# More staging, value and bias-table tiles around the attention; modulation sums without a cleared accumulator, closed three steps later

## The chip, the cores and the metric

The kernel runs on one core of one Trainium2 chip. The metric is the device time of one execution in microseconds (us), taken as the median of several runs. Before the change it is 2842.87 us, the median of 3 runs between 2839.62 and 2844.02 us.

Names of the engines: PE is TensorE (matmuls; PEld are its weight loads), DVE is VectorE, ACT is ScalarE, POOL is GpSimd, SP is SyncE, which here only issues DMAs. SPq and ACTq are the DMA queues that SP and ACT feed.

## The reference, cut to what matters

The model has two layers over 256 latent tokens and 256 context tokens with 2048 features, all in float32. Every layer first turns a conditioning vector into six modulation vectors of 2048 values:

```
sh1, sc1, g1, sh2, sc2, g2 = split(silu(c) @ ada_w[l] + ada_b[l], 6)
h = rmsnorm(x) * (1 + sc1) + sh1
layer 0: y = concat(gated_delta_net(h, ctx), neighbourhood_attention(h, ctx)) @ w_out
layer 1: y = (gate_b * conv3(gate_c * val)) @ w_out
x = x + g1 * y
x = x + g2 * swiglu(rmsnorm(x) * (1 + sc2) + sh2)
out = rmsnorm(x)
```

The gated-DeltaNet half has 8 heads. For each it inverts 64x64 triangles and then runs a recurrence over chunks, forward and backward, first over the context and then over the latent tokens. The attention half has 8 heads: 256 queries against 256 latent keys within a window, with a learned bias table (`ev_rpb`), and against 256 context keys, in one softmax.

## The kernel before, in words

**Matmuls.** Every weight matrix comes from HBM in tiles of 128x1024 float32 (`raw`, L226, four buffers in layer 0's first half). ACT makes a rounded copy `whi` (L169), DVE the remainder `wlo` (L238), and PE multiplies three of the four products of the high and low parts (L284 to L295 and L309 to L313). These streams are called QB, KB, VB, ZA, W_out and so on by the columns of the weight matrix.

**Modulation vectors.** The six vectors of layer 0 that are not needed at once, and those of layer 1, are summed in the background by `ada_job`. For a block of columns (512 wide in layer 0's first half, 1024 wide later) POOL clears `acc` (128 x width, L327), a DMA puts the bias of the block in its first row (L328), and 16 steps follow: a DMA loads `araw` (L331, three buffers for the narrow form), and DVE adds `araw` times a column of silu(c) to `acc` (L332). Then the block is closed at once: PE sums `acc` over the partitions. For 512 columns these are 4 products with a column of ones (L338); for 1024, `acc` is split into high and low part and goes through 16 products (L346), and ACT takes the row out of PSUM (`grow`). There are 12 narrow and 14 wide blocks.

**Staging.** The streams QB, KB and VB end in `stage`: ACT or DVE copies a 128x512 result out of PSUM into a tile `nst` (L1050, L164, L166), and an ACT queue DMA stores it in HBM (L1051). ZA does the same with `zst` (L1118 to L1121), under the same tag. There are `NST` = 2 such tiles.

**Attention.** Per head, `na_scores` loads the windows of the bias table with two DMAs on the ACT queue into `br` (one buffer, L1081), DVE adds the band mask and writes `bq` (two buffers, L1084), and PE forms the scores (L1088) and adds the bias (L1089). `na_values` loads `vb` (two buffers, L1103) and forms the output (L1112).

**Recurrence.** A latent step is, on PE, state times keys (L918), state times queries (L927), `xdT` times `R` (L938), in some steps the state update (L946), and `AT` times `vn` (L960). Between them DVE makes `R` (L921) and ACT makes `vd` and `vn` (L942, L956).

**What sets the order.** Nothing in the program fixes the order of an engine's instructions: a scheduler with its own timeline puts them in order when the kernel is built, by what each needs and when its buffer comes free. Each engine then executes its list strictly in that order, so an instruction that waits holds all behind it, and so does a DMA issue in its queue.

Of the kernel before, what the change touches and what calls it, by code (L numbers as in the profile page):

```python
# [23 lines left out]
F32 = mybir.dt.float32  # L24
F32R = mybir.dt.float32r
AF = mybir.ActivationFunctionType
OP = mybir.AluOpType
AX = mybir.AxisListType

D = 2048  # L30
KT = D // 128
# [8 lines left out]
GH = 6  # L40
YO = (2, 0, 1, 3)
NPT = 1
AB = 3
R_QB = 1.2
R_KB = 1.8
R_ZA = 1.8
R_WO = 2.0
NST = 2
TAIL = 2
HEAD = 2  # L50
PO = 96
# [54 lines left out]
def body(tc, x, c, ctx, c_ctx, ada_w, ada_b, norm_mix, norm_ffn, ffn_w_gate, ffn_w_up, ffn_w_down,  # L106
# [3 lines left out]
    PE, ACT, DVE, POOL, SP = nc.tensor, nc.scalar, nc.vector, nc.gpsimd, nc.sync  # L110
# [43 lines left out]
    def smt():  # L154
        small.append(small.pop(0))
        return small[0].tile([128, 512], F32, name="sm", tag="sm")
# [11 lines left out]
    def acopy(dst, src):  # L168
        ACT.activation(dst, src, AF.Copy)  # L169
# [12 lines left out]
    ident = C("ident")  # L182
    pick = cpool.tile([128, 15], F32R, name="pick")
    ones = C("ones")

    def transpose(dst, src):
        n = src.shape[0]
        return PE.transpose(dst, src, ident[:n, :n])  # L188

    cT = cpool.tile([128, 32], F32, name="cT")  # L190
# [6 lines left out]
    gcol = {}  # L197
    row_d = {}
# [118 lines left out]
            yield  # L317


    def ada_job(pool_, l, seg, kind, gamma=None, width=1024, bufs=2):  # L320

        wr = ada_w[l].rearrange("(k p) n -> p k n", p=128)
        nf = width // 128
        for blk in range(D // width):
            c0 = seg * D + blk * width
            acc = pool_.tile([128, width], F32, name="acc", tag="acc", bufs=1)
            POOL.memset(acc, 0.0)  # L327
            SP.dma_start(acc[0:1, :], ada_b[l:l + 1, c0:c0 + width])  # L328
            for k in range(KT):
                raw = pool_.tile([128, width], F32, name="araw", tag="araw", bufs=bufs)  # L330
                SP.dma_start(raw, wr[:, k, c0:c0 + width])  # L331
                DVE.scalar_tensor_tensor(acc, raw, cT[:, k:k + 1], acc, op0=OP.mult, op1=OP.add)  # L332
                yield
            fs_ = slice(blk * nf, (blk + 1) * nf)
            p = smt()
            if width < 1024:
                for f in range(nf):
                    PE.matmul(p[:, f:f + 1], acc[:, f * 128:(f + 1) * 128], ones[:, 0:1], start=True, stop=True)  # L338
                pc = p
            else:  # L340
                ah = pool_.tile([128, width], F32R, name="ah", tag="ah", bufs=1)
                al = pool_.tile([128, width], F32R, name="al", tag="al", bufs=1)
                split(ah, al, acc, DVE)
                for f in range(nf):
                    for a in (ah, al):
                        PE.matmul(p[0:nf, 0:128], pick[:, nf - 1 - f:2 * nf - 1 - f], a[:, f * 128:(f + 1) * 128],  # L346
                                  start=f == 0 and a is ah, stop=f == nf - 1 and a is al)
                g = pool_.tile([16, 128], F32, name="grow", tag="grow", bufs=1)[0:nf]
                acopy(g, p[0:nf, 0:128])
                if kind == "row":  # L350
                    ACT.dma_start(row_d[l, seg][fs_], g)
                    continue
                pc = smt()
                transpose(pc[:, 0:nf], g)
            if kind == "sc":
                DVE.scalar_tensor_tensor(scc[l, seg - 1][:, fs_], pc[:, 0:nf], 1.0, gamma[:, fs_], op0=OP.add, op1=OP.mult)
            else:
                DVE.tensor_copy((shc if kind == "sh" else gcol)[l, seg][:, fs_], pc[:, 0:nf])
        if kind == "row" and width < 1024:
            p = smt()  # L360
            transpose(p[0:16, 0:128], gcol[l, seg])
            g = pool_.tile([16, 128], F32, name="grow", tag="grow", bufs=1)
            DVE.tensor_copy(g, p[0:16, 0:128])
            SP.dma_start(row_d[l, seg], g)

    def load_row(l, seg):
        r = rpool.tile([128, D], F32, name="row", tag="row", bufs=1)
# [3 lines left out]

    class Pump:
        def __init__(self, jobs, steps, total):
            self.it = (s for j in jobs for s in j)
            self.rate = total / max(steps, 1)
            self.due = 0.0
            self.done = False
# [62 lines left out]
    p = smt()  # L440
# [621 lines left out]
    nap = pool("na", stack=nastk)  # L1062
# [3 lines left out]
    bandf = C("band")  # L1066
# [6 lines left out]
    def na_scores(h):  # L1073
        kb = nap.tile([128, 512], F32, name="kb", tag="kb", bufs=2)
        qb = nap.tile([128, 256], F32, name="qb", tag="qb", bufs=2)
        bq = nap.tile([128, 6, 64], F32, name="bq", tag="bq", bufs=2)
        br = nap.tile([128, 6, 64], F32, name="br", tag="br", bufs=1)
        for half in range(2):
            src = bass.AP(tensor=ev_rpb.tensor, offset=ev_rpb.offset + h * 465 + (5 - half) * 31 + 15 - 63,
                          ap=[[1, 64], [31, 6], [1, 64]])  # L1080
            ACT.dma_start(br[half * 64:half * 64 + 64], src)  # L1081
        SP.dma_start(kb, kb_d[:, h, :])
        SP.dma_start(qb, qb_d[:, h, :])
        DVE.tensor_tensor(bq, br, bandf[:, None, :].to_broadcast([128, 6, 64]), op=OP.add)  # L1084
        out_ = []
        for t in range(2):
            p = nat(h)
            PE.matmul(p, qb[:, t * 128:(t + 1) * 128], kb, start=True, stop=False)  # L1088
            PE.matmul(p[:, 0:256], C("flip"), bq[:, 2 - 2 * t:6 - 2 * t, :].rearrange("p s c -> p (s c)"),  # L1089
                      start=False, stop=True)  # L1090
            s = nap.tile([128, 512], F32, name="s", tag="s", bufs=4)
            m = nap.tile([128, 1], F32, name="m", tag="m", bufs=4)
            DVE.tensor_reduce(m, p, axis=AX.X, op=OP.max, negate=True)
            l = nap.tile([128, 1], F32, name="l", tag="l", bufs=4)
            ACT.activation(s, p, AF.Exp, bias=m, accum_out=l)
            DVE.reciprocal(l, l)
            DVE.tensor_scalar(s, s, l, None, op0=OP.mult)
            out_.append(s)
        return out_

    def na_values(h, ss):
        vb = nap.tile([128, 4, 128], F32, name="vb", tag="vb", bufs=2)
        SP.dma_start(vb, vb_d[:, :, h * 128:(h + 1) * 128])  # L1103
        PT = nap.tile([128, 4, 256], F32, name="PT", tag="PT", bufs=NPT)
        for t in range(2):
            pt = nat(h)
            for j in range(4):
                transpose(pt[:, j * 128:(j + 1) * 128], ss[t][:, j * 128:(j + 1) * 128])
            copy(PT[:, :, t * 128:(t + 1) * 128], pt.rearrange("p (j q) -> p j q", j=4))
        po = nat(h)  # L1110
        for j in range(4):
            PE.matmul(po[:, 0:256], vb[:, j, :], PT[:, j, :], start=j == 0, stop=j == 3)  # L1112
        split(yhi[2 + h // 4][:, h % 4, :], ylo[2 + h // 4][:, h % 4, :], po[:, 0:256])
# [98 lines left out]
    row = []  # L1212
# [191 lines left out]
```

## Time and profile before

| | |
|---|---|
| median of 3 runs | 2842.87 us (2839.62 to 2844.02) |
| the profiled execution | 2848.17 us, span 2846.4 us |
| PE busy in the span | 2732.5 us, 96% |
| DVE, ACT, POOL busy | 68%, 46%, 2% |
| mean granted TensorE clock | 0.986 of full speed |

The span is what the profiler saw from the first instruction to the last. The profiled execution takes 1.8 us more than its span and lies 5.3 us above the median. A "busy" matmul is counted with its pipeline, and its end is modelled, so PE may lose a little more than its idle time says. In square brackets behind a row stands how long the engine was idle before it and what released it.

### The profile page before, as it was taken

To read this page: it belongs to the slowest core of one execution; us is meant where nothing else is said; L and a number is where in the kernel's file an instruction comes from. 1 tells how busy PE (TensorE), PEld (TensorE's weight loads), DVE (VectorE), ACT (ScalarE), POOL (GpSimd) and SP (SyncE) were. 2 spreads that over 40 slices of the span, in tenths; PEclk is the share of its full clock that TensorE was granted. 3 is DMA by queue.
4 is the path that set the end of the run, shared out by engine and by line. 5 is a ranking of instruction groups with operands and counts; after the bars stand their busy time and mean duration, and the time that the engine had idled before them with its cause. 6 is when DMAs were issued, how large, how long until landed. Compare 5 with 4: busy or idle time off the path is not lost.

```text
span 2846.4 us, 40363 instructions
## 1 busy us (share of the span) xinstructions
PE 2732.5 (96%) x15113; PEld 2281.6 (80%) x15113; DVE 1924.8 (68%) x2647; ACT 1308.3 (46%) x1945; POOL 51.1 (2%) x77
## 2 busy tenths in 40 slices
PE   5999999989989999999999999999999999999998
PEld 3699989888767778888888878878878888888886
DVE  3387767857667878776677768897678644445665
ACT  3267543222354544444445545444454444444554
POOL 0000001000000000000000000000000000000000
PEclk9999999999999999999999999999999999999999
DMA  9955568777758599987788657998559766656653
GB/s 345 311 177 164 143 208 253 243 225 236 210 170 278 200 318 346 347 285 249 272 305 282 198 175 243 328 319 306 179 179 332 262 188 180 195 186 215 192 192 126
DMA packets 284927, 680.78 MB, mean 239 GB/s; under 512 B 57273, under 2 KB 97313, under 8 KB 283323
## 3 DMA queue, kind: packets, MB, share of 16 engines
q1 hardware_dynamic: 262148, 652.48, 69.4%
q10 hardware_dynamic: 22583, 25.73, 3.0%
q8 instruction: 118, 1.93, 0.3%
q14 instruction: 78, 0.64, 0.1%
HBM read 657.63 MB, written 20.48 MB: 238 GB/s over the span
## 4 chain that ended last, share of the span: by engine, by line
PE 70%; DMA 15%; DVE 9%; issue 3%; ACT 2%; SPq 1%; POOL 0%; ACTq 0%; DVEq 0%; POOLq 0%
PE mm L287 17%; PE mm L285 17%; PE mm L284 17%; DMA araw<-in_ada_w_dram 11%; PE mm L313 7%; DVE acc L332 3%; DVE wlo L238 3%; PE sm L188 2%; PE mm L293 2%; PE mm L295 2%; PE mm L294 2%; DMA raw<-in_od_w_in_dram 1%; DMA acc<-in_ada_b_dram 1%; PE gd L477 1%; ACT whi L169 0%
## 5 line engine op out<-in xcount | busy, mean ns | idle before, releaser
L238 DVE TENSOR_TENSOR wlo<-raw,whi 128x1024 fp32r<-128x1024 f32 x800 | 971.5, 1222 | 452.3 <-ACT whi L169 446.3
L169 ACT ACTIVATE whi<-raw 128x1024 fp32r<-128x1024 f32 x800 | 841.9, 1058 | 875.5 <-PE mm L287 632.4
L332 DVE SCALAR_TENSOR_TENSOR acc<-araw,cT,acc 128x1024 f32<-128x1024 f32 (+1 forms) x416 | 431.2, 1037 | 228.4 <-DMA araw<-in_ada_w_dram 198.8
L285 PE MATMUL mm<-wlo,fhi 128*128 128x512 f32 x1232 | 473.6, 394 | 0.2 <-DVE wlo L238 0.2
L284 PE MATMUL mm<-whi,fhi 128*128 128x512 f32 x1232 | 470.9, 396 | 0.6 <-ACT fhi L1187 0.6
L287 PE MATMUL mm<-whi,flo 128*128 128x512 f32 x1232 | 392.2, 392 | 0.1
L284 PEld LDWEIGHTS mm<-whi,fhi 128*128 128x128 f32 x1232 | 232.4, 189 | 50.4 <-ACT fhi L1187 1.0
L287 PEld LDWEIGHTS mm<-whi,flo 128*128 128x128 f32 x1232 | 231.0, 188 | 50.7 <-DVE flo L1189 0.3
L285 PEld LDWEIGHTS mm<-wlo,fhi 128*128 128x128 f32 x1232 | 232.5, 189 | 48.7 <-DVE wlo L238 0.7
L284 PE MATMUL mm<-whi,ahi 128*128 128x512 f32 x672 | 259.8, 392 | 0.0
L285 PE MATMUL mm<-wlo,ahi 128*128 128x512 f32 x672 | 259.4, 391 | 0.0
L287 PE MATMUL mm<-whi,alo 128*128 128x512 f32 x672 | 209.7, 392 | 0.0
L313 PE MATMUL mm<-hllo,whi 128*128 128x256 f32 x640 | 181.1, 287 | 0.0
L313 PE MATMUL mm<-hlhi,wlo 128*128 128x256 f32 x600 | 169.4, 288 | 2.0 <-issue 1.5
L313 PE MATMUL mm<-hlhi,whi 128*128 128x256 f32 x600 | 167.5, 290 | 1.0 <-DVE hlhi L502 1.0
L172 ACT ACTIVATE ahi<-prodT 128x256 fp32r<-128x256 f32 x176 | 73.0, 417 | 194.7 <-PE mm L285 187.6
L285 PEld LDWEIGHTS mm<-wlo,ahi 128*128 128x128 f32 x672 | 126.2, 188 | 27.5
L284 PEld LDWEIGHTS mm<-whi,ahi 128*128 128x128 f32 x672 | 126.2, 188 | 27.2
L287 PEld LDWEIGHTS mm<-whi,alo 128*128 128x128 f32 x672 | 126.1, 188 | 27.3
L285 PE MATMUL mm<-wlo,dhi 128*128 128x512 f32 x336 | 127.3, 398 | 2.6 <-DVE wlo L238 2.4
L313 PEld LDWEIGHTS mm<-hllo,whi 128*128 128x128 f32 x640 | 124.0, 194 | 0.4
L284 PE MATMUL mm<-whi,dhi 128*128 128x512 f32 x336 | 123.5, 396 | 0.3 <-DVE u_t L1329 0.3
(399 smaller groups left out, 4055.9 us busy)
## 6 DMA issues: line engine op xcount, KB each, us to landing
araw<-in_ada_w_dram SPq DMA_DIRECT2D x288, 512.0 KB
raw<-in_ffn_w_down_dram SPq DMA_DIRECT2D x176, 512.0 KB
raw<-in_ffn_w_gate_dram SPq DMA_DIRECT2D x160, 512.0 KB
raw<-in_ffn_w_up_dram SPq DMA_DIRECT2D x160, 512.0 KB
raw<-in_ev_w_in_dram SPq DMA_DIRECT2D x112, 512.0 KB
araw<-in_ada_w_dram SPq DMA_DIRECT2D x192, 256.0 KB
raw<-in_od_w_in_dram SPq DMA_DIRECT2D x96, 512.0 KB
raw<-in_ev_w_out_dram SPq DMA_DIRECT2D x32, 512.0 KB
```

The lines of the kernel that those rows point to most:

```text
L169: ACT.activation(dst, src, AF.Copy)
L172: ACT.activation(hi, src, AF.Copy)
L188: return PE.transpose(dst, src, ident[:n, :n])
L238: DVE.tensor_tensor(lo, raw, hi, op=OP.subtract)
L284: PE.matmul(ps[ti][n], a, hi[:, n * 512:(n + 1) * 512], start=first, stop=False)
L285: PE.matmul(ps[ti][n], a, lo[:, n * 512:(n + 1) * 512], start=False, stop=False)
L287: PE.matmul(ps[ti][n], b, hi[:, n * 512:(n + 1) * 512], start=False, stop=False)
L293: PE.matmul(ps[ti][n], lh(t), hi[:, c_], start=False, stop=False)
L294: PE.matmul(ps[ti][n], lh(t), lo[:, c_], start=False, stop=False)
L295: PE.matmul(ps[ti][n], ll(t), hi[:, c_], start=False, stop=hi is group[-1][0])
L313: PE.matmul(ps[f][:, n * 256:(n + 1) * 256], wt, mv(w, k), start=False, stop=i == len(ks) - 1 and g == len(group) - 1 and j == 2 and w == ...
L332: DVE.scalar_tensor_tensor(acc, raw, cT[:, k:k + 1], acc, op0=OP.mult, op1=OP.add)
```

## The change

It has four parts.

1. **More tiles**: `NST` from 2 to 4 (`nst`, `zst`), `vb` from 2 to 3 buffers.
2. **Bias tables**: the two DMAs per head go to the SP queue and write straight into `bq` (three buffers); DVE adds the mask in place. `br` is gone.
3. **No cleared accumulator**: the first product of a block writes `acc` (a tensor_scalar, no add), and the block's bias comes as a small tile `abias` of its own. For narrow blocks PE adds it with one product of `abias` and the identity; for wide ones DVE adds it when it takes the sum out of PSUM, which ACT did before without the bias.
4. **Closing later**: a narrow block is closed in step `LAG` = 3 of the next block, with two `acc` tiles in turn. `in_order` closes the last block.

```diff
-NST = 2
+LAG = 3
+NST = 4
@@ ada_job
-            acc = pool_.tile([128, width], F32, name="acc", tag="acc", bufs=1)
-            POOL.memset(acc, 0.0)
-            SP.dma_start(acc[0:1, :], ada_b[l:l + 1, c0:c0 + width])
-            for k in range(KT):
-                raw = pool_.tile([128, width], F32, name="araw", tag="araw", bufs=bufs)
-                SP.dma_start(raw, wr[:, k, c0:c0 + width])
-                DVE.scalar_tensor_tensor(acc, raw, cT[:, k:k + 1], acc, op0=OP.mult, op1=OP.add)
-                yield
+        def close(blk, acc, bias):
+            if width < 1024:
+                PE.matmul(p[:, 0:nf], bias, ident[0:nf, 0:nf], start=True, stop=False)
                 for f in range(nf):
-                    PE.matmul(p[:, f:f + 1], acc[:, f * 128:(f + 1) * 128], ones[:, 0:1], start=True, stop=True)
+                    PE.matmul(p[:, f:f + 1], acc[:, f * 128:(f + 1) * 128], ones[:, 0:1], start=False, stop=f == nf - 1)
...
-                acopy(g, p[0:nf, 0:128])
+                DVE.tensor_tensor(g, p[0:nf, 0:128], bias, op=OP.add)
...
+        for blk in range(nblk):
+            c0 = seg * D + blk * width
+            acc = pool_.tile([128, width], F32, name="acc", tag="acc", bufs=1 if width == 1024 else 2)
+            bias = pool_.tile([16, 128], F32, name="abias", tag="abias", bufs=1 if width == 1024 else 2)[0:nf]
+            SP.dma_start(bias, ada_b[l, c0:c0 + width].rearrange("(f p) -> f p", p=128))
+            for k in range(KT):
+                raw = pool_.tile([128, width], F32, name="araw", tag="araw", bufs=bufs)
+                SP.dma_start(raw, wr[:, k, c0:c0 + width])
+                col = cT[:, k:k + 1]
+                if k:
+                    DVE.scalar_tensor_tensor(acc, raw, col, acc, op0=OP.mult, op1=OP.add)
+                else:
+                    DVE.tensor_scalar(acc, raw, col, None, op0=OP.mult)
+                if k == LAG and closing:
+                    closing.pop()()
+                yield
+            if width == 1024:
+                close(blk, acc, bias)
+            else:
+                closing.append(lambda a=(blk, acc, bias): close(*a))
+
+    def in_order(jobs):
+        for j in jobs:
+            yield from j
+        for _ in range(LAG):
+            yield
+        if closing:
+            closing.pop()()
@@ na_scores
-        bq = nap.tile([128, 6, 64], F32, name="bq", tag="bq", bufs=2)
-        br = nap.tile([128, 6, 64], F32, name="br", tag="br", bufs=1)
+        bq = nap.tile([128, 6, 64], F32, name="bq", tag="bq", bufs=3)
...
-            ACT.dma_start(br[half * 64:half * 64 + 64], src)
+            SP.dma_start(bq[half * 64:half * 64 + 64], src)
...
-        DVE.tensor_tensor(bq, br, bandf[:, None, :].to_broadcast([128, 6, 64]), op=OP.add)
+        DVE.tensor_tensor(bq, bq, bandf[:, None, :].to_broadcast([128, 6, 64]), op=OP.add)
@@ na_values
-        vb = nap.tile([128, 4, 128], F32, name="vb", tag="vb", bufs=2)
+        vb = nap.tile([128, 4, 128], F32, name="vb", tag="vb", bufs=3)
```

Since the scheduler orders the instructions anew, the four parts move more than their own lines. Three places matter below. "xN" is a run of N equal instructions.

On POOL, while the triangles are solved (`n` are copies out of a triangle, `xdT`, `xd`, `zsol` cleared tiles), the list before was this:

```order
L859 MEMSET xdT 128x2048 x2
L327 MEMSET acc 128x512
L815 COPY n_1950<-nt 32x128 x16
L831 MEMSET zsol 128x1024
L832 MEMSET zsol 128x32
L858 MEMSET xd 128x1024 x2
L327 MEMSET acc 128x512
```

and now is:

```order
L886 MEMSET xdT 128x2048 x2
L842 COPY n_1950<-nt 32x128 x16
L858 MEMSET zsol 128x1024
L859 MEMSET zsol 128x32
L885 MEMSET xd 128x1024 x2
```

Before, the second block of modulation sums could not begin until POOL had reached the second `acc` behind the solve. Now nothing of the sums stands in POOL's list.

At the start of the attention, the bias tables before stood in ACT's list, between the last stores of VB (`vb_d`) and the weight copies `whi`:

```order
L164 ACTIVATE nst<-mm 128x512
L1051 DMA vb_d<-nst 128x512
L1081 DMA br<-in_ev_rpb_dram 64x6x64 x2
L1051 DMA vb_d<-nst 128x512
L169 ACTIVATE whi<-raw 128x1024 x3
L1081 DMA br<-in_ev_rpb_dram 64x6x64 x2
```

Now they stand in SP's list, ahead of each head's keys and queries (`kb`, `qb`) and of the weight tiles (`raw`):

```order
L1107 DMA bq<-in_ev_rpb_dram 64x6x64 x2
L1108 DMA kb<-kb_d 128x512
L1109 DMA qb<-qb_d 128x256
L1107 DMA bq<-in_ev_rpb_dram 64x6x64 x2
L1108 DMA kb<-kb_d 128x512
L1109 DMA qb<-qb_d 128x256
L1129 DMA vb<-vb_d 128x4x128
L1107 DMA bq<-in_ev_rpb_dram 64x6x64 x2
L1129 DMA vb<-vb_d 128x4x128 x2
L227 DMA raw<-in_ev_w_in_dram 128x1024 x2
```

Three tables are now asked for before the first weight tile of that stretch.

On PE, the last latent step before had stream matmuls (`mm`) among its parts:

```order
L960 MATMUL gd<-vn,AT 128x128 x4
L918 MATMUL gd<-state,kT 128x128 x4
L188 MATMUL sm<-cs,s 128x128 x4
L295 MATMUL mm<-whi,hllo 128x512
L293 MATMUL mm<-whi,hlhi 128x512
L294 MATMUL mm<-wlo,hlhi 128x512
L295 MATMUL mm<-whi,hllo 128x512
L927 MATMUL gd<-state,qT 128x128 x4
L938 MATMUL gd<-R,xdT 128x128 x4
L1112 MATMUL sm<-PT,vb 128x256 x4
L1088 MATMUL sm<-kb,qb 128x512
L1089 MATMUL sm<-bq,cs 128x256
```

and now the last two follow one another, and a third stands ahead of them with only small products of the attention in it:

```order
L987 MATMUL gd<-vn,AT 128x128 x4
L945 MATMUL gd<-state,kT 128x128 x4
L954 MATMUL gd<-state,qT 128x128 x4
L965 MATMUL gd<-R,xdT 128x128 x4
L987 MATMUL gd<-vn,AT 128x128 x4
L945 MATMUL gd<-state,kT 128x128 x4
L954 MATMUL gd<-state,qT 128x128 x4
L965 MATMUL gd<-R,xdT 128x128 x4
L987 MATMUL gd<-vn,AT 128x128 x4
L1114 MATMUL gd<-kb,qb 128x512
```

The streams run ahead of the recurrence by more than before, and are used up before its last three steps.

## Rows read from the trace of the kernel before

**Rows 1.** Page, part 1: busy us, share of the span, instructions of each engine.
```profile
PE 2732.5 (96%) x15113; PEld 2281.6 (80%) x15113; DVE 1924.8 (68%) x2647; ACT 1308.3 (46%) x1945; POOL 51.1 (2%) x77
```
**Rows 2.** Busy time by stretch: length, PE, PEld, DVE, ACT, POOL, clock, DMA share, GB/s.
```profile
400.00:700.00 300.00, 281.08 (x2598) 259.06 (x2597) 214.01 (x387) 94.14 (x173) 20.55 (x31) 0.97 0.78 243
700.00:775.00 75.00, 67.98 (x354) 55.55 (x353) 48.23 (x92) 26.66 (x59) 0.00 (x0) 0.95 0.78 228
775.00:860.00 85.00, 76.07 (x373) 59.21 (x372) 50.81 (x114) 48.80 (x113) 0.53 (x1) 0.96 0.50 156
860.00:1000.00 140.00, 134.27 (x591) 108.43 (x591) 107.86 (x158) 69.58 (x102) 1.49 (x2) 0.98 0.73 246
1000.00:1700.00 700.00, 697.10 (x3171) 570.36 (x3170) 511.00 (x506) 329.20 (x400) 7.26 (x9) 1.00 0.81 280
```
**Rows 3.** Timeline of PE (start, us, what): the starts that end its longer gaps.
```profile
508.40 0.83 PE L338 MATMUL sm<-cs,acc 128*128 128x1 f32 x6 [1.99 <-DVE acc L332]
...
575.47 0.79 PE L309 MATMUL mm<-h,whi 128*128 128x512 f32 x1 [5.10 <-DVE nst L166]
...
586.15 0.95 PE L887 MATMUL gd<-xdT,Y 32*32 32x32 f32 x53 [3.84 <-ACT Y L169]
...
720.60 0.73 PE L284 MATMUL mm<-whi,hlhi 128*128 128x512 f32 x2 [3.50 <-ACT whi L169]
...
738.92 1.22 PE L1089 MATMUL sm<-bq,cs 128*128 128x256 f32 x2 [3.40 <-DVE bq L1084]
```
**Rows 4.** Timeline of ACT and its queue around 715 us.
```profile
712.37 2.35 ACTq L1081 DMA_DIRECT2D br<-in_ev_rpb_dram  x2
719.12 0.32 ACTq L1051 DMA_DIRECT2D vb_d<-nst  x1
719.49 2.95 ACT L169 ACTIVATE whi<-raw 128x1024 fp32r<-128x1024 f32 x3 [8.49 <-DMA br<-in_ev_rpb_dram]
```
**Rows 5.** Timeline of DVE at 738 us.
```profile
738.31 0.56 DVE L1084 TENSOR_TENSOR bq<-br,cs 128x384 f32<-128x384 f32 x1 [6.48 <-DMA br<-in_ev_rpb_dram]
```
**Rows 6.** Timeline of DVE around 575 us.
```profile
570.54 0.75 DVE L332 SCALAR_TENSOR_TENSOR acc<-araw,cT,acc 128x512 f32<-128x512 f32 x1 [5.50 <-DMA araw<-in_ada_w_dram]
...
574.73 0.68 DVE L166 COPY nst<-mm 128x512 f32<-128x512 f32 x1
...
583.01 0.75 DVE L332 SCALAR_TENSOR_TENSOR acc<-araw,cT,acc 128x512 f32<-128x512 f32 x1 [3.84 <-DMA araw<-in_ada_w_dram]
```
**Rows 7.** Timeline of PE: the last latent step.
```profile
804.55 1.06 PE L918 MATMUL gd<-state,kT 128*128 128x128 f32 x8
...
808.46 1.16 PE L938 MATMUL gd<-R,xdT 128*128 128x128 f32 x8 [0.59 <-DVE R L921]
...
814.32 0.91 PE L960 MATMUL gd<-vn,AT 128*128 128x128 f32 x6 [1.68 <-DVE o_t L932]
```
**Rows 8.** Timeline of ACT in the same step.
```profile
811.82 0.60 ACT L1118 ACTIVATE zst<-mm 128x512 f32<-128x512 f32 x1 [5.17 <-DMA zd<-zst]
...
813.54 1.14 ACT L956 ACTIVATE vn<-gd,beta 128x128 f32<-128x128 f32 x4 [1.13 <-DVE zst L1120]
```
**Rows 9.** Groups by line and shape: count, busy us, mean ns, idle before.
```profile
L332 DVE SCALAR_TENSOR_TENSOR acc<-araw,cT,acc 128x1024 f32<-128x1024 f32 x224 | 287.4, 1283 | 133.8 <-DMA araw<-in_ada_w_dram 124.1 <-DMA acc<-in_ada_b_dram 6.0 <-issue 0.9
...
L332 DVE SCALAR_TENSOR_TENSOR acc<-araw,cT,acc 128x512 f32<-128x512 f32 x192 | 143.8, 749 | 94.6 <-DMA araw<-in_ada_w_dram 74.7 <-DMA acc<-in_ada_b_dram 11.5 <-issue 6.0
```
**Rows 10.** The tensor_scalar over 2048 columns: ns (least, median, most), first and last start.
```profile
L516 DVE TENSOR_SCALAR xn<-xn,n0r x4: 1281/1282/1286, 36.3 to 39.9; 128x2048 f32<-128x2048 f32 x4
```
**Rows 11.** Waits of SP's queue, 700 to 860 us: total, times, longest.
```profile
SPq L1103 <- PE sm L1112: 26.3, 5, 12.4
...
SPq L331 <- DMA br<-in_ev_rpb_dram: 5.0, 2, 3.6
```
**Rows 12.** DMA queues, 712 to 745 us (q1 SP, q10 ACT): packets, MB, share.
```profile
q1 hardware_dynamic: 4066, 7.22, 65.9%
q10 hardware_dynamic: 2537, 1.14, 19.2%
```

More of the change, by code (lines that the diff above doesn't have):

```diff
@@ L317, in fm_stream @@
             yield
+    closing = []
     def ada_job(pool_, l, seg, kind, gamma=None, width=1024, bufs=2):
@@ L323, in ada_job @@
         nf = width // 128
-        for blk in range(D // width):
-            c0 = seg * D + blk * width
-            acc = pool_.tile([128, width], F32, name="acc", tag="acc", bufs=1)
-            POOL.memset(acc, 0.0)
-            SP.dma_start(acc[0:1, :], ada_b[l:l + 1, c0:c0 + width])
-            for k in range(KT):
-                raw = pool_.tile([128, width], F32, name="araw", tag="araw", bufs=bufs)
-                SP.dma_start(raw, wr[:, k, c0:c0 + width])
-                DVE.scalar_tensor_tensor(acc, raw, cT[:, k:k + 1], acc, op0=OP.mult, op1=OP.add)
-                yield
+        nblk = D // width
+        def close(blk, acc, bias):
             fs_ = slice(blk * nf, (blk + 1) * nf)
@@ L348, in ada_job @@
                 g = pool_.tile([16, 128], F32, name="grow", tag="grow", bufs=1)[0:nf]
-                acopy(g, p[0:nf, 0:128])
+                DVE.tensor_tensor(g, p[0:nf, 0:128], bias, op=OP.add)
                 if kind == "row":
                     ACT.dma_start(row_d[l, seg][fs_], g)
-                    continue
+                    return
                 pc = smt()
@@ L358, in ada_job @@
                 DVE.tensor_copy((shc if kind == "sh" else gcol)[l, seg][:, fs_], pc[:, 0:nf])
[L359 to L364, printed above, removed]
+            if kind == "row" and blk == nblk - 1:
+                p = smt()
+                transpose(p[0:16, 0:128], gcol[l, seg])
+                g = pool_.tile([16, 128], F32, name="grow", tag="grow", bufs=1)
+                DVE.tensor_copy(g, p[0:16, 0:128])
+                SP.dma_start(row_d[l, seg], g)
+        for blk in range(nblk):
[25 more added lines that the diff above has]
+            closing.pop()()
     def load_row(l, seg):
@@ L373, in __init__ @@
         def __init__(self, jobs, steps, total):
-            self.it = (s for j in jobs for s in j)
+            self.it = in_order(jobs)
             self.rate = total / max(steps, 1)
```

## The prediction

> **What bounds the kernel now.** I read the page first: PE is busy 2732.5 of 2846.4 us, so all that a change can win without taking matmuls away is some 114 us of PE idle time [rows 1]. Next the busy time by stretch, to see where that idle time lies [rows 2]: subtract PE's figure from the length. It is 18.9 us in 400 to 700, 7.0 in 700 to 775, 8.9 in 775 to 860, 5.7 in 860 to 1000, and only 2.9 in the 700 us after that, where PE is simply full. The start of the kernel, which is not touched, holds much of the rest. So work that the change takes off DVE, ACT or POOL behind 1000 us is worth next to nothing, and the argument is about the 40.5 us of the four stretches between 400 and 1000. Then PE's timeline there, for the single gaps and what ended them [rows 3], and last the timelines of the engines named, since the releaser of a gap is often only the messenger [rows 4 to 6].
>
> A measurement of this kernel can tell some 0.2% (5.7 us) from no change.
>
> **The change part by part.**
>
> *Bias tables.* Two gaps belong to them. PE waits 3.50 us for a `whi` at 720.60 [rows 3]; ACT made it late, because it stood 8.49 us behind the issue of two `br` loads and a store in its own list [rows 4]. PE waits 3.40 us at 738.92 for a `bq`, and DVE says why: it had stood 6.48 us for a `br`, whose one buffer lets the next load start only when the mask of the head before is added [rows 3, 5]. In the changed order no table stands in ACT's list, and three are asked for before the attention's first weight tile. Both gaps go: 6.9 us. The bounds are 0 (a table in SP's line is as late as one in ACT's) and the 7.0 us that PE idles in this stretch at all [rows 2]; I take 6.9, because three tables ahead is more than the 6.48 us that one was late.
>
> *Staging.* Only one gap is surely the buffers': in the last latent step ACT waits 5.17 us at 811.82 for the store of an earlier `zst`, its `vn` comes behind that, and PE's AT product starts 1.68 us late [rows 7, 8]. With four tiles the four ZA results need no store to finish: 1.7 us. The larger gap, 5.10 us at 575.47, names the copy into `nst` [rows 3]. But DVE got to that copy only at 574.73, after standing 5.50 us in front of an `araw` that had not landed; and the 3.84 us before 586.15 follow a second such stand, of 3.84 us, at 583.01 [rows 6]. More `nst` tiles do not move an `araw`. I take 0 for these two, with 0 and 8.9 us gained as bounds.
>
> *Third value buffer.* SP stands 26.3 us in 5 waits before a `vb` load until the head two before is done, with weight tiles behind it [rows 11]. PE shows no long gap for it; I take 0, and its part in the 8.9 us of the stretch is a bound.
>
> *Closing later.* One gap is a closing that came too early: 1.99 us at 508.40 [rows 3]. Three steps later the sum is long there: 2.0 us. Against it stand 12 more products (4x128). Their price is not in the trace; the nearest row is the closing product itself, six in 0.83 us, or 0.14 us each [rows 3]. Twelve cost 1.7 us; the bounds are 0 (hidden in a gap) and twice that.
>
> *No clearing, bias apart.* The first product becomes a tensor_scalar. Four of these over 2048 columns took 1.28 us each [rows 10], so 0.64 for 1024 and 0.32 for 512 against 1.283 and 0.749 [rows 9]: DVE saves 14 x 0.64 + 12 x 0.43 = 14.1 us, and no longer stands for the 4 KB bias row, 11.5 + 6.0 us [rows 9]. Most of it lies beside a full PE. The row taken out of PSUM moves from ACT to DVE, 14 short instructions, also beside a full PE. I take 0. If that cover went, all 31.6 us would count, but PE's idle time there is 2.9 us [rows 2].
>
> *What the order does besides.* Without POOL's clearing the sums start earlier, and half of the steps that stood beside W_out are gone from there (16 instead of 32). The stretch 860 to 1000 has 5.7 us of idle time to give; I take 0, since DMA there is busy 73% [rows 2] and the end of W_out waits for the norm in any case. On the other side the recurrence moves back against the streams: its last three steps have no stream matmul between their parts. Before, the last step took from 804.55 to 814.32, that is 9.8 us, for four groups of about 1 us each, so some 4.1 us of PE's own work [rows 7]. The bare chain is shorter: key product 1.1, `R` about as long, `xdT` product 1.2, `vn` 1.1 [rows 7, 8], so some 4.5 us from first product to AT, and the missing 5.3 are stands like the store's, which the change removes. An uncovered step then idles some 0.5 to 5.7 us; I take 0.5 x 3 = 1.5 and give the same 1.5 back, since the three attention steps that covered it before now find the streams earlier. Net 0, bounds -8.9 (all idle time of the stretch [rows 2]) and +17.1 (three steps at 5.7).
>
> *Sum.* -6.9 - 1.7 - 2.0 + 1.7 = -8.9 us. The profiled execution is 2848.17 us (2846.4 of span and 1.8 around it), which gives 2839.3; it lies 5.3 us above the median, so for the median 2842.87 - 8.9 = 2834 us. With the bounds of the small terms this case runs from 2826 to 2838.
>
> **The rivals.**
>
> *A. DVE's stands go too.* If the sums, freed from POOL, find their `araw` landed, the 8.9 us of the two gaps at 575 and 586 go as well [rows 3, 6]: 2825, and with the idle time of 860 to 1000 down to 2819. For it: the sums spread over more time. Against it: in 400 to 700 as many steps stand as before, DMA is busy 78% [rows 2], and `araw` keeps three buffers.
>
> *B. Given back.* Each gap closes and another opens, since DVE and ACT stand in strict order: 2842, between 2837 and 2848. For it: PE's gap at 575.47 was three waits deep [rows 3, 6]; where one releaser goes the next is often close behind.
>
> *C. The bare recurrence (slower).* Place: the last three latent steps. Price: if each takes 9.8 us as before with 4.1 of work [rows 7], 3 x 5.7 = 17.1 us, so 2851. It decides from the point where a step takes more than 4.1 + 3.0 = 7.1 us, for then the three eat the 8.9 gained. For it: nothing else is left for PE but short products of the attention. Against it: a stand of 5.17 us in that very step is one that the change removes [rows 8].
>
> *D. The tables in SP's line (slower).* A pair of table loads is 2 x 96 KB in runs of 256 B, 768 packets. ACT's queue moved 2537 packets in 19.2% of 33 us of 16 engines, 40 ns each [rows 12], so one pair holds all engines 1.9 us, ahead of the weight tiles behind it. Eight pairs: 15.4 us, so 2849 if PE feels all of it. Against it: four weight tiles are loaded ahead, DMA is busy only 50% in 775 to 860 [rows 2], and SP stands for buffers there, not for data [rows 11]. The Trainium skill, "DMA: Bandwidth & Descriptors", section "Queues, rings and completion order", says that each DMA engine takes turns between the queues that have work and consumes each queue's descriptors in ring order. By that rule a table on ACT's queue shared the engines with the weights, while on SP's it stands before them, which is this rival; the rows show both queues moving in the same 33 us, and none shows a table within SP's line.
>
> **How the numbers follow.** The forecast has 0.44, A 0.14, B 0.22, C 0.14, D 0.06. Faster by over 0.2% is below 2837.2: 0.38 of the forecast, all of A, 0.02 of B, together 0.54. Slower is above 2848.6: 0.12 of C, 0.05 of D, 0.03 of B, together 0.20. Within 0.2% remain 0.26. The range 2818 to 2851 holds the forecast, B, nearly all of A and D and half of C; the likeliest case alone runs from 2826 to 2838.
>
> **What would show it.** Right: no ACT or DVE wait for a `bq` load, no PE gap at the first table products, no wait of `zst` for a store, no PE wait at the closings, and still stands of DVE for `araw` of 3 to 5 us between 400 and 700. C: latent steps of over 7 us with PE gaps behind `R` and `vn`. D: `whi` waiting for a `raw` behind a table. Wrong altogether: PE idle time above 42 us between 400 and 1000 with the named gaps gone, or a change of more than 3 us behind 1000.

## The result, and the profile after

The changed kernel is slower: 2858.34 us, the median of 6 runs (2851.92 to 2860.07), against 2843.44 (2839.62 to 2846.58) for the kernel before beside it. The ratio is 1.005, with a 95% interval of 1.0037 to 1.0062. The forecast was 2834, its range ended at 2851, and the direction was wrong. The profiled execution took 2859.7 us.

Page, part 1, of the changed kernel; it answers to [rows 1]:

```profile
PE 2740.3 (96%) x15137; PEld 2290.8 (80%) x15137; DVE 1916.4 (67%) x2661; ACT 1306.0 (46%) x1932; POOL 31.6 (1%) x51
```

DVE and POOL have less to do, as the change intends, and PE is busy 7.8 us longer. The same five stretches as in [rows 2] (length, PE, PEld, DVE, ACT, POOL, clock, DMA share, GB/s):

```profile
400.00:700.00 300.00, 280.17 (x2748) 256.15 (x2747) 200.88 (x363) 91.29 (x161) 17.66 (x24) 0.95 0.79 247
700.00:775.00 75.00, 66.89 (x337) 54.17 (x337) 51.20 (x87) 26.20 (x50) 0.00 (x0) 0.98 0.77 233
775.00:860.00 85.00, 78.28 (x442) 65.84 (x441) 47.76 (x104) 41.08 (x97) 0.00 (x0) 0.96 0.51 161
860.00:1000.00 140.00, 130.57 (x585) 104.04 (x584) 100.68 (x179) 73.01 (x136) 0.00 (x0) 0.98 0.56 186
1000.00:1700.00 700.00, 699.73 (x3191) 573.35 (x3190) 510.24 (x511) 330.82 (x395) 0.00 (x0) 1.00 0.81 284
```

PE idles 44.1 us in the first four, against 40.6. That is 3.5 us more, and the kernel lost 15, so these stretches do not hold the loss as idle time. The place is found by one event that both kernels have: the first transposes of the norm behind layer 0's attention, in PE's timeline (start, us, what) of before, after, and the kernel one_acc told of below:

```profile
943.86 1.11 PE L188 MATMUL sm<-cs,xc 128*128 128x128 f32 x4 [3.81 <-DVE nx1v L212]
```

```profile
964.65 2.82 PE L189 MATMUL sm<-cs,xc 128*128 128x128 f32 x12 [4.35 <-DVE xc L1204]
```

```profile
938.35 0.66 PE L189 MATMUL sm<-cs,xc 128*128 128x128 f32 x4 [4.35 <-DVE xc L1204]
```

In these two traces, which lie 11.5 us apart, the loss lies ahead of it: 20.8 us. Behind it 9 us come back: the stretch from there to the next such norm shrank from 762.9 to 756.9 us and the one behind that from 381.9 to 378.3. Of the 6.0 us in the first, PE's idle time gave 2.8 and its busy time 3.2, with the same products (busy time in that stretch, before and after):

```profile
943.90:1706.80 762.90, 755.02 (x3423) 617.24 (x3423) 559.76 (x595) 367.12 (x466) 8.23 (x10) 0.99 0.79 272
```

```profile
964.60:1721.50 756.90, 751.81 (x3422) 615.50 (x3422) 556.62 (x601) 365.79 (x457) 0.57 (x2) 1.00 0.79 274
```

Busy time is not work alone, for the granted clock differs. Ahead of the norm PE idles 6.8 us longer (84.2 us before, 91.0 after) and is busy 14.0 us longer (859.7 and 873.6). The products of `abias` hold at most 4.8 of that. By the clock records of the traces, 39 us of the busy time before and 53 after were at the lower level, 1.2 GHz. There 128x512 products start 0.43 us apart instead of 0.23 (before, at 946.5 and at 953.0), so these 14 us more cost some 7 us, an estimate. In both traces PE's longest gaps behind the first 60 us, eight before and seven after, each have such a stretch at their end. Here are the one behind the gap of 5.10 us [rows 3], before, and the one at the gap of 7.08 us shown below, after:

```profile
575.00:578.40 3.40, 2.93 (x12) 2.83 (x13) 0.87 (x2) 2.57 (x6) 0.00 (x0) 0.50 0.79 202
```

```profile
626.80:637.00 10.20, 8.39 (x93) 7.75 (x94) 3.29 (x5) 0.38 (x1) 0.00 (x0) 0.50 0.74 154
```

Behind the norm it is the other way round: 23 us of the busy time before and 12 after were at the lower level, so some 5 of the 9 us that come back are the clock's, by the same estimate.

Of PE's named gaps [rows 3] none is left at its place; others have opened (timeline of PE, after):

```profile
408.92 0.58 PE L310 MATMUL mm<-h,whi 128*128 128x256 f32 x1 [3.24 <-ACT nst L1077]
...
628.61 0.28 PE L907 MATMUL gd<-xd,n 32*32 32x32 f32 x2 [7.08 <-DMA xd<-dz]
...
811.77 1.44 PE L954 MATMUL gd<-state,qT 128*128 128x128 f32 x5 [4.73 <-DVE o_t L989]
...
868.95 1.53 PE L1138 MATMUL gd<-PT,vb 128*128 128x256 f32 x3 [3.67 <-ACT PT L165]
```

The recurrence is late as a whole. DVE's timeline has the copy that ends each of the two triangle solves; before, and after:

```profile
366.11 1.15 DVE L840 COPY lsol<-zsol 128x1024 f32<-128x1024 f32 x1
...
558.05 1.12 DVE L840 COPY lsol<-zsol 128x1024 f32<-128x1024 f32 x1
```

```profile
400.23 1.16 DVE L867 COPY lsol<-zsol 128x1024 f32<-128x1024 f32 x1
...
613.25 1.08 DVE L867 COPY lsol<-zsol 128x1024 f32<-128x1024 f32 x1
```

The solves end 34 and 55 us later, and the last latent steps come 44 us later, at 848 to 859 us instead of up to 814 [rows 7]. Here they are, on PE, after:

```profile
848.31 1.05 PE L987 MATMUL gd<-vn,AT 128*128 128x128 f32 x8
849.20 1.06 PE L945 MATMUL gd<-state,kT 128*128 128x128 f32 x8
850.21 1.16 PE L954 MATMUL gd<-state,qT 128*128 128x128 f32 x8
851.48 1.16 PE L965 MATMUL gd<-R,xdT 128*128 128x128 f32 x8
853.09 1.26 PE L987 MATMUL gd<-vn,AT 128*128 128x128 f32 x8 [0.46 <-ACT vn L983]
...
858.21 1.26 PE L987 MATMUL gd<-vn,AT 128*128 128x128 f32 x8 [0.52 <-ACT vn L983]
```

The stream that covered them (ZA) starts its last product at 806.6 us in both kernels: it is the recurrence that is later, and not the stream that is earlier. The bare steps themselves are short, 4.8 and 5.1 us; what costs is that the products that need their result begin so much later, with no stream beside them. W_out shows it: 48 of its 384 products are done near 834 us before, near 841 after. The rest begin only behind the first transposes of the recurrence's output (`o_t`, at 853.4 and 873.6 us); before, and after:

```profile
857.19 0.48 PE L284 MATMUL mm<-whi,yhi 128*128 128x512 f32 x1
```

```profile
877.98 0.48 PE L285 MATMUL mm<-whi,yhi 128*128 128x512 f32 x1
```

That is 20.8 us later, as the norm is, and the norm starts 86.7 us behind this point in both (85 to 88 in all the kernels below). The last AT product lies 42 us ahead of it before, but only 19 after.

### The profile page after: what moved, and what is told of

Its sections match the earlier page's. It is cut to its first block, busy times and chain, and to the rows that moved or that the text cites. A ratio compares the mean times of both kernels' runs of the same rounds, so it can differ in the third digit from the quotient of the medians.

```text
span 2857.9 us, 40351 instructions
## 1 busy us (share of the span) xinstructions
PE 2740.3 (96%) x15137; PEld 2290.8 (80%) x15137; DVE 1916.4 (67%) x2661; ACT 1306.0 (46%) x1932; POOL 31.6 (1%) x51
## 4 chain that ended last, share of the span: by engine, by line
PE 78%; DMA 12%; DVE 5%; ACT 3%; issue 2%; SPq 1%; DVEq 0%; ACTq 0%
PE mm L288 19%; PE mm L286 19%; PE mm L285 19%; PE mm L314 8%; DMA araw<-in_ada_w_dram 6%; PE mm L296 2%; PE mm L294 2%; PE mm L295 2%; PE sm L189 2%; DMA bq<-in_ev_rpb_dram 1%; DVE acc L374 1%; DVE wlo L239 1%; DMA raw<-in_ev_w_in_dram 1%; DMA dz<-lsol 1%; DMA raw<-in_od_w_in_dram 1%
## 5 line engine op out<-in xcount | busy, mean ns | idle before, releaser
L374 DVE SCALAR_TENSOR_TENSOR acc<-araw,cT,acc 128x1024 f32<-128x1024 f32 (+1 forms) x390 | 404.2, 1036 | 203.1 <-DMA araw<-in_ada_w_dram 198.8
L288 PE MATMUL mm<-whi,alo 128*128 128x512 f32 x672 | 209.6, 392 | 0.0
```

The costliest lines, as they stand in the source:

```text
L288: PE.matmul(ps[ti][n], b, hi[:, n * 512:(n + 1) * 512], start=False, stop=False)
L374: DVE.scalar_tensor_tensor(acc, raw, col, acc, op0=OP.mult, op1=OP.add)
```

## The experiments

Three theories. **Theory 1**: the second narrow `acc` tile is what lets sums run ahead. With one tile a block's first sum waits until the block before is closed. With two, the order puts 32 sums ahead of the end of the first solve and 128 ahead of the second, where before 16 and 87 stood. DVE works through its list in order, so the solves are late. **Theory 2**: the bias tables wait in SP's line (rival D). **Theory 3**: the new way to sum and close costs by itself. In each trace three things were read: the start of the copy that ends the second solve; DVE's time for sums, busy plus its waits for `araw`, before and behind 560 us; and the start of that norm. These three are of one profiled execution each, which lies up to 6.5 us from its kernel's median. Waits for anything else, such as the bias rows of the kernel before, are not in the sums' columns. With all waits the sums of 150 to 800 us take 200.0 us before, 201.6 after and 209.6 in all_but_sums, which is faster than before; so this total does not rank the kernels, and Theory 1 rests on how many sums stand ahead of which step.

| kernel | median us | ratio to before (95%) | solve 2 | sums 150-560, 560-800 | norm |
|---|---|---|---|---|---|
| before | 2842 to 2845 | 1 | 558 | 91, 93 | 943.9 |
| after | 2858.3 | 1.0050 (1.0037-1.0062) | 613 | 118, 83 | 964.6 |
| one_number | 2856.7 | 1.0053 (1.0035-1.0071) | 610 | 110, 83 | 956.1 |
| one_acc | 2833.6 | 0.9964 (0.9950-0.9977) | 558 | 98, 84 | 938.4 |
| all_but_sums | 2839.3 | 0.9983 (0.9972-0.9995) | 551 | 86, 101 | 942.5 |
| held | 2857.4 | 1.0046 (1.0029-1.0062) | 589 | 94, 102 | 968.4 |
| held_twice | 2848.4 | 1.0012 (0.9998-1.0026) | 554 | 80, 132 | 958.7 |
| held_thrice | 2843.1 | 1.0004 (0.9990-1.0017) | 571 | 94, 84 | 950.1 |
| one_acc_late | 2857.3 | 1.0035 (1.0021-1.0050) | 615 | 97, 106 | 967.7 |
| one_acc_held | 2847.4 | 1.0012 (1.0000-1.0023) | 518 | 60, 131 | 957.2 |
| one_acc_end | 2835.0 | 0.9971 (0.9959-0.9983) | 561 | 96, 67 | 937.8 |
| one_acc_act | 2834.8 | 0.9970 (0.9956-0.9984) | 562 | 95, 87 | 941.8 |
| one_acc_own_tables | 2834.6 | 0.9972 (0.9962-0.9983) | 554 | 93, 82 | 932.9 |
| tables_only | 2847.5 | 1.0017 (1.0006-1.0029) | 561 | 93, 91 | 947.1 |
| stage_only | 2837.0 | 0.9988 (0.9977-1.0000) | 549 | 87, 92 | 933.7 |
| sums_one_tile | 2841.7 | 1.0000 (0.9988-1.0011) | 563 | 96, 81 | 949.6 |

**One number changed in the kernel before** (one_number):

```diff
-            acc = pool_.tile([128, width], F32, name="acc", tag="acc", bufs=1)
+            acc = pool_.tile([128, width], F32, name="acc", tag="acc", bufs=1 if width == 1024 else 2)
```

> The kernel before with one number changed: two acc tiles in turn instead of one for the narrow blocks, still cleared by POOL, biased by the 4 KB row and closed at once. In the built order this alone moves 16 more sums ahead of the first triangle solve and leaves the last three latent steps without stream matmuls, as in the changed kernel. Theory 1 (the second acc tile lets the sums run ahead, and the recurrence is late): 2858 us, 1.005 of before. Theory 2 (the bias tables in SP's line cost the time): 2843, no change. Theory 3 (the new way of closing, bias product and first product cost it): 2843, no change.

It is as slow as the whole change, with POOL's clearing, the old tables and two `nst` tiles. So the clearing did not hold the sums back; the one tile did. In the trace of the kernel before it is POOL that waits, 313.8 us in nine places, until the closing products of a block let it clear the tile; and sums_one_tile below, without clearing, keeps 16 sums ahead of the first solve, as before.

**The whole change with one tile** (one_acc), which needs the block closed at once (the edit in effect):

```diff
-            acc = pool_.tile([128, width], F32, name="acc", tag="acc", bufs=1 if width == 1024 else 2)
+            acc = pool_.tile([128, width], F32, name="acc", tag="acc", bufs=1)
-            if width == 1024:
-                close(blk, acc, bias)
-            else:
-                closing.append(lambda a=(blk, acc, bias): close(*a))
+            close(blk, acc, bias)
```

> The changed kernel with one acc tile for the narrow blocks, and so closed at once; no clearing, bias tile, four staging tiles, three value tiles and tables on SP stay. Its built order has the recurrence where the kernel before has it. Theory 1: faster than before by the small terms of the prediction, 2834 to 2838 us (0.997 to 0.998). Theory 2: still slow, 2855. Theory 3: partly slow, 2850.

With three variants below that agree with it within the intervals it is the fastest of all, and faster than both kernels. In the changed kernel the second tile, with the late closing that it allows, turns a gain of 0.36% into a loss of 0.50%.

**Without the sums' part** (all_but_sums): the kernel before with four `nst`, three `vb` and the tables on SP's queue; `ada_job` as it was.

> The kernel before with the staging tiles, the third value tile and the tables on SP straight into bq, and the modulation sums as before. Theory 1: faster than before by what the prediction gave these three, some 8 us: 2835 (0.997). Theory 2: 2855 (1.004). Theory 3: 2835.

This removes Theory 2 as the cause of the loss: with the tables in SP's line the kernel is faster than before.

**Two tiles, sums held back by the order.** In the changed kernel a block's first sum may be placed only behind a given instruction: in held, block 2 behind the first solve; in held_twice also block 6 behind the second; in held_thrice block 7 instead of 6, and block 11 behind the last latent step (the lines condensed):

```diff
+    if len(held_) == 2: order.enter_context(tc.issue_after(solved[0].ins))      # held
+    at = {2: 0, 6: 1}.get(len(held_))                                           # held_twice
+    at = {2: 0, 7: 1}.get(len(held_))                                           # held_thrice
+    if len(held_) == 11: order.enter_context(tc.issue_after(latent[-1].ins))    # held_thrice
```

> The changed kernel, two acc tiles and late closing kept, but the first product of the second narrow block is ordered behind the end of the first triangle solve on DVE. In the built order 16 sums stand ahead of that solve, as before the change, 112 ahead of the second (before 87, changed 128), and the last latent step still has a little stream work. Theory 1 (the sums ahead of the solve, not the tile or the closing as such): most of the loss is gone, 2840 to 2848. Theories 2 and 3: no better than the changed kernel, 2855 to 2858.

A miss. The first solve was on time again (370 us), but 112 sums stood ahead of the second, which ended 31 us late; the kernel was as slow as the changed one.

> The changed kernel whole (two sums tiles, closing three steps late), but the sums of the second and of the sixth 512-column block may start only behind the first and the second triangle solve, so that about as many sums stand ahead of either solve as in the kernel before (16 and 80 there, against 32 and 128 in the changed kernel; 16 and 112 in the kernel 'held'). Theory 1, mended after 'held' (what counts is the number of sums ahead of either solve, the second as much as the first, because what the solve ends late the recurrence is late at its end): second solve's end near 560 us instead of 589, the first product of the last latent step near 815 us, and 2833 to 2842 us. Theory 3 (two tiles and the late closing cost by themselves, wherever the sums stand): 2852 to 2860 us, as 'held' and the changed kernel.

Both solves were on time, and the loss fell from 0.50% to 0.12%, short of Theory 1's range and below Theory 3's. Its trace says what was still wrong. DVE's sums between 560 and 800 us, in groups (count, busy us, mean ns, idle before), before and in held_twice:

```profile
L332 DVE SCALAR_TENSOR_TENSOR acc<-araw,cT,acc 128x512 f32<-128x512 f32 x73 | 54.7, 749 | 49.6 <-DMA araw<-in_ada_w_dram 38.7 <-DMA acc<-in_ada_b_dram 7.4 <-issue 2.6
```

```profile
L376 DVE SCALAR_TENSOR_TENSOR acc<-araw,cT,acc 128x512 f32<-128x512 f32 x88 | 66.0, 750 | 63.7 <-DMA araw<-in_ada_w_dram 62.5
```

With the 5 first products, 93 sums stand there instead of 73, and each brings its wait for 256 KB of weights: 132 us of DVE in a stretch of 240, where before 93 us went (104 with its other waits). What was taken from the solves was put on the latent steps. Between 150 and 800 us held, held_twice, one_number and the changed kernel all have 175 sums, the kernel before and one_acc 159 and 157. The second tile brings one block more.

> The changed kernel whole (two sums tiles, closing three steps late), with the second 512-column block of sums held behind the first triangle solve, the seventh behind the second, and the eleventh behind the last latent steps: 16 and 96 sums ahead of the solves and 160 until the recurrence ends, as in the kernel before (16, 87, 160) and in one_acc (16, 92, 160). Theory 1, in its last form (the second tile costs because one more block of 16 sums, with VectorE's waits for their weight rows, falls within 150 to 800 us): VectorE's sums and their waits in that stretch come back from 200 to 212 us to 180 to 190, and the time to 2832 to 2842 us. Theory 3 (two tiles and the late closing cost by themselves): 2846 to 2858 us, as 'held_twice' and 'held'.

With that block put off, DVE's sums take 178 us in 150 to 800 us (before: 183), as Theory 1 said, and the time is back at that of before, 1.1 us above the range given. All of the loss against before is gone with two tiles and the late closing kept. But 9.4 us remain against one_acc; the second solve ends 12 us later there, and whether that is all was not settled. Against held_twice two things changed at once, the block held behind the second solve and the one behind the last latent step, and no run takes them apart.

**Useless work ahead of the solves** (one_acc_late): one_acc with 16 useless operations ahead of each solve, whose result is overwritten.

```diff
+        for _ in range(16):
+            DVE.scalar_tensor_tensor(sub_tmp, cs[:, 0:512], cT[:, 0:1], cs[:, 512:1024], op0=OP.mult, op1=OP.add)
```

> The kernel one_acc (all of the change but with one sums tile, closed at once) with 16 more VectorE operations of 128x512 ahead of each triangle solve; their result is overwritten, they are work that is not needed. At the 0.7 us that such an operation takes in the rows of the kernels before it, that is 11 us of VectorE ahead of either solve, with no block of sums moved by hand. Theory 1 (lateness of the solves is what costs; where it comes from does not matter): last latent step 12 to 22 us later than in one_acc (810 us), three latent steps behind the end of the streamed products, and 2842 to 2856 us. Theory 3 (the cost lies in how the sums are added and closed, not in when the solves end): within 4 us of one_acc, 2830 to 2838 us.

The second solve ends at 615 us, the last AT product starts at 861 (51 us later than in one_acc, where 12 to 22 had been expected), and 24 us are lost by the medians (20 by the ratios), 1 us above the range, for 24.0 us of DVE work by the trace:

```profile
L862 DVE SCALAR_TENSOR_TENSOR sub_tmp<-cs,cT 128x512 f32<-128x512 f32 x32 | 24.0, 751 | 0.4
```

So time on DVE ahead of the solves costs, whatever fills it: one tile and closing at once do not protect. But the edit is not clean: the order changed with it. The solves end 25 and 56 us later than in one_acc for 12 and 24 us of useless work, and 107 sums stand ahead of the second instead of 92. Ahead of the first the number stayed at 16, so there it is other work than sums that made the solve late.

**Fewer sums, earlier or later** (one_acc_held: block 3 behind the second solve; one_acc_end: block 10 behind the last latent step; edits as above).

> The kernel one_acc with one edit: the sums of the third 512-column block may start only behind the second triangle solve, so that 32 sums stand ahead of it instead of 92. Theory 1: the second solve ends some 35 to 40 us earlier (60 operations of 0.65 us) if VectorE is what it waits for, the last latent step moves forward with it, and what is won is bounded by the idle time that is left of TensorE there: 2822 to 2832 us. Rival: the sums that are put off come due behind the streams and close the last modulation columns late, so that the first matrix product behind the norm waits; 2836 us or more.

The solve ended 40 us earlier, as both sides had it, and the kernel lost 13.7 us: the rival's direction, but not its mechanism, since the sums did not come due behind the streams. They filled the latent steps' stretch:

```profile
L376 DVE SCALAR_TENSOR_TENSOR acc<-araw,cT,acc 128x512 f32<-128x512 f32 x105 | 78.7, 749 | 50.4 <-DMA araw<-in_ada_w_dram 49.1
```

With 6 first products that is 131 us again in 560 to 800 us, and 12 us of PE idle time in 700 to 800. The balance counts, not the solve alone.

> The kernel one_acc with the tenth 512-column block of sums held behind the last latent steps: 144 sums until the recurrence ends instead of 160; both solves as in one_acc. If VectorE's time in that stretch is what bounds it further: 16 sums with their waits less, some 15 to 20 us of VectorE, 3 to 10 us off the time, 2824 to 2831 us. If one_acc is already bounded by TensorE there, or the block that is put off comes due before the norm: 2832 to 2842 us.

18 us of DVE less in 560 to 800 us than in one_acc, and no gain: one_acc is no longer bound by it. W_out's later products begin 40 us behind the last AT product in one_acc, against 19 in the changed kernel; what holds them there was not tested.

**The parts that the forecast priced.** tables_only, stage_only (four `nst`, three `vb`) and sums_one_tile (the new sums with one tile, closed at once) are single parts of the diff put into the kernel before; in one_acc_act the tables are issued by ACT, in one_acc_own_tables they are loaded as before:

```diff
-            SP.dma_start(bq[half * 64:half * 64 + 64], src)
+            ACT.dma_start(bq[half * 64:half * 64 + 64], src)     # one_acc_act
+            ACT.dma_start(br[half * 64:half * 64 + 64], src)     # one_acc_own_tables, with br
```

> The kernel before with one edit of the change: the bias tables go by SP's queue straight into three buffers, without ScalarE's additions' source tile. The prediction's largest term by itself (6.9 us, the two stands of TensorE for these tables): 2836 to 2839 us against 2844. If VectorE waits for the tables in SP's line in the place of it: 2841 to 2849 us.

The tables alone lose 0.17%. DVE's group for the mask, before and in tables_only (count, busy, mean ns, idle before):

```profile
L1084 DVE TENSOR_TENSOR bq<-br,cs 128x384 f32<-128x384 f32 x8 | 4.4, 554 | 11.9 <-DMA br<-in_ev_rpb_dram 11.9
```

```profile
L1083 DVE TENSOR_TENSOR bq<-bq,cs 128x384 f32<-128x384 f32 x8 | 4.5, 559 | 22.0 <-DMA bq<-in_ev_rpb_dram 22.0
```

DVE stands for a table 22 us instead of 11.9, although there are three buffers. The edit changes the queue, the tile that is loaded and the buffers at once.

> The kernel before with two edits of the change: four stage buffers instead of two and three value buffers instead of two; nothing else. The prediction priced them at a gain of 1.7 us: 2840 to 2843 against 2842 to 2844. If the gain of all_but_sums (about 5 us, with a tables' part that costs up to 5) is theirs: 2832 to 2838 us.

A gain of 0.12% by the ratio (3.4 us), with an interval that reaches 1.0000, and 4.9 us by the medians: perhaps more than the 1.7 priced. The gap of 5.10 us [rows 3] that was held to be an `araw`'s is gone; in its trace that product waits 0.46 us:

```profile
572.52 0.50 PE L309 MATMUL mm<-h,whi 128*128 128x512 f32 x1 [0.46 <-ACT nst L164]
```

> The kernel before with the new sums alone (first product by itself without clearing, bias as a product of its own, no memset), with one sums tile and closed at once; stage, value and bias buffers as before. The prediction priced closing and bias products at 0.3 us together: within 3 us of before. If one_acc's gain over all_but_sums (5.6 us) is theirs: 2835 to 2839 us.

No change, as priced. Its trace does not say why: there the norm is 5.7 us later than before and the two stretches behind it are 6.0 and 5.6 us shorter, so that this trace is 5.7 us shorter than that of before, where the medians agree. The clock is part of it, since PE's busy time behind the norm holds 15 us at the lower level there and 23 before.

> The kernel one_acc with one edit: the eight bias tables, which the change loads by SP's queue, are issued by ACT's queue, straight into the same three buffers. Theory 2 (in SP's line a table stands behind the weight streams, and VectorE stands for it): VectorE's waits for these loads, 30 us in one_acc, fall below 12, and the time falls by 2 to 8 us, to 2826 to 2832 us. Against it: these waits of VectorE lie beside streamed products that TensorE has ahead, and the time stays within 2 us of one_acc (2833.6), or ACT's line gives them back to the chunks' evictions.

> The kernel one_acc with the bias tables as in the kernel before (a source tile of their own, loaded by ACT's queue, two buffers of the result). If the tables' part costs 4 to 6 us wherever it stands (tables_only): 2826 to 2831 us, the fastest version. If it costs only beside two stage buffers, or the stands of TensorE that the prediction counted come back: 2833 to 2840 us.

Neither moves the time. In one_acc the tables' waits (30.2 us on SP's queue, 11.7 with `br`) lie beside a PE that has work. On ACT's queue, into the same three buffers, they are 23.5 us and not below 12 as expected, so SP's queue explains 6.7 of the 18.5 us between the two forms, and the rest stays open. The tables cost only in the kernel with two stage buffers; why the parts do not add up (0.9988 and 1.0017 alone, 0.9983 together) stays open.

## Why the prediction was wrong

**The step that failed** is "what the order does besides", priced at "net 0". It saw that the sums start earlier and that the recurrence moves back, but took POOL's clearing for what had held the sums, and looked for the cost in the last three bare steps alone. The runs put in its place: the second `acc` tile lets one more block of 16 sums into 150 to 800 us; DVE pays for a sum's wait as well as for its work, so the solves, or the latent steps, are late, and with them W_out's later products. In the two traces that is the delay of 20.8 us of the norm, the slower clock included; by the medians the whole loss is 14.9 us. one_number shows that the second tile costs it by itself, and held_thrice takes it back; the 9.4 us that it stays behind one_acc are open.

**Rival C** had the right sign and place and the wrong mechanism. A bare step takes 5 us, not 9.8, some 0.9 us over its own work of 4.1. Three of them explain 3 us, not 17.

**Bias tables, -6.9.** Both gaps went, but the condition given for it, no DVE wait for a `bq`, failed: DVE waits 23.8 us in the changed kernel, 1.8 to 2.5 us even for the first tables, and PE idles 8.1 us in 700 to 775 instead of 7.0 [rows 2]:

```profile
719.05 0.56 DVE L1110 TENSOR_TENSOR bq<-bq,cs 128x384 f32<-128x384 f32 x1 [1.84 <-DMA bq<-in_ev_rpb_dram]
723.14 0.56 DVE L1110 TENSOR_TENSOR bq<-bq,cs 128x384 f32<-128x384 f32 x1 [1.79 <-DMA bq<-in_ev_rpb_dram]
727.96 0.56 DVE L1110 TENSOR_TENSOR bq<-bq,cs 128x384 f32<-128x384 f32 x1 [2.53 <-DMA bq<-in_ev_rpb_dram]
```

Alone it is +4.8 us (0.0017 of 2842). Rival D thus named a real cost, a third of its 15.4 us, and not the cause of the result. The rule that it names (the Trainium skill, "DMA: Bandwidth & Descriptors", "Queues, rings and completion order") agrees in direction with the 6.7 us by which DVE waits longer on SP's queue than on ACT's (one_acc and one_acc_act); no run here tells it apart from a later issue of the tables.

**Staging, -1.7.** The store's wait of `zst` [rows 8] is gone as said. The value may have been too small, since stage_only won 3.4 to 4.9 us, with an interval that reaches no gain. The 5.10 us, taken at 0, went with the buffers too: in its trace DVE still stands for an `araw` there, 4.32 us ahead of 577.19, and PE has no such gap. That both a stand of DVE and a full ring of tiles were needed for it is argued from this, not shown.

**Closing and bias products, -0.3.** No PE wait at a closing is left, and sums_one_tile measured 0. The products take 4.8 us of PE's busy time for 12 blocks, not 1.7, and the first product saves DVE less than a tensor_scalar of [rows 10] promised:

```profile
L334 PE MATMUL sm<-cs,abias 4*128 4x4 f32 x24 | 4.8, 266 | 0.0
```

```profile
L376 DVE TENSOR_SCALAR acc<-araw,cT 128x1024 f32<-128x1024 f32 x14 | 10.5, 750 | 3.7 <-DMA araw<-in_ada_w_dram 3.5
...
L376 DVE TENSOR_SCALAR acc<-araw,cT 128x512 f32<-128x512 f32 x12 | 5.8, 479 | 2.8 <-DMA araw<-in_ada_w_dram 2.8
```

**Behind 1000 us, "next to nothing".** Both signs that the prediction named for being wrong altogether came as numbers: over 42 us idle with the named gaps gone, and over 3 us behind 1000. But the second does not speak against this term. The trace of the changed kernel is 9.3 us shorter behind the norm, some 5 of them by the estimate from the clock, and one_number, in which nothing is changed there, takes the same time behind its norm, 1893.6 us against 1893.3 (before 1902.5).

one_acc, the change without its second tile, came to 2833.6 us, the time that the sum of the terms had given for the whole. That is chance: three of the terms were mis-sized, with both signs.

## What to carry to other kernels

A second buffer for background work is no free relaxation where a scheduler fills gaps: the one buffer may be what holds that work back, and an in-order engine then pays for its loads as well. Before pricing such a change, compare how many background instructions stand ahead of each step of the longest chain in the two orders, and price each at its duration plus its wait. Then take the parts alone: here the buffer that lost and the buffers that gained stood in the same diff.

## What the runs showed that was not expected

- A long gap of PE is paid twice in these traces: as idle time, and as busy time at 1.2 GHz at its end, where the clock stays low for 3.4 to 10.2 us. So a loss can stand in busy time. In the changed kernel's trace most of the 20.8 us does; in one_number's, where 32 us of the busy time ahead of the norm were at the lower level, all 12 us are idle time.
- A tensor_scalar over 1024 and 512 columns took 750 and 479 ns, where [rows 10] had 1281 for 2048: not in proportion to the columns.
- Loads of 192 KB in small pieces on SP's queue, straight into three buffers, kept DVE standing nearly twice as long as on ACT's queue with a tile of their own (11.9 to 22.0 us); beside one `acc` tile, into three buffers in both cases, it was 23.5 us on ACT's queue and 30.2 on SP's, so the queue is the smaller part.
